# Query-key scores on one core: blocks of 8 heads, loads of 64 partitions of 8 KB, three output buffers

## The chip, the cores and the metric

One core of a Trainium2 chip. The metric is the device time of one execution in microseconds, the median of several runs. The granted TensorE clock was 1.0 in every profile.

Names used below, with what nearly all the work of each is on the page of the kernel before: PE multiplies matrices (1536 MATMUL at L159), DVE (vector) transposes (92 STREAM_TRANSPOSE), ACT (scalar) copies PE's results into the output buffers (379 COPY o_sb<-ps at L170), POOL casts (352 CAST at L115), and SP issues transfers (the 96 stores and a few first loads). A partition is one of the 128 rows of a tile (128x2048 in a copy of ACT); a packet is one transfer in the profile's records of the sixteen DMA engines (28248 in the kernel before).

## The reference

```python
batch, n_heads, seq, head_dim = 8, 12, 1024, 64
def reference(q, k):                      # float32
    return np.einsum('bhid,bhjd->bhij', q, k)
```

There are 96 heads. Each reads 2 x 256 KB and writes 4 MB.

## The kernel before

Heads are worked in blocks: two of 2 heads, then blocks of 4 (two "halves" of GMAX = 2 heads). For each block, q and k are loaded in rows of 4 KB per partition, cast to fp16 on POOL, transposed on DVE, multiplied on PE, evicted by ACT into an output buffer of 32 KB per partition, and stored with one 4 MB DMA per head.

```python
GMAX = 2
sizes = [1, 1] + [GMAX] * (BH // (2 * GMAX) - 1)
in_pool   = ...tile_pool(name="in_pool", bufs=5)
half_pool = ...tile_pool(name="half_pool", bufs=2)
out_pool  = ...tile_pool(name="out_pool", bufs=4)
...
def load(self, n, eng):                       # one of q, k for one half of a block
    half, x = divmod(n, 2)
    ...
    eng.dma_start(out=self.raw[half][:, x],   # 128 partitions x 4 KB
                  in_=src.rearrange("(p r) d -> p (r d)", p=P))
...
for i, b in enumerate(blocks):
    for n in range(2 * b.G):
        b.scores(n, side)                     # matmuls, evictions, store; side: DVE transposes
        if i == n == 0:
            next_load(nc.scalar)
        next_load(nc.scalar)                  # one load per head, on ACT's queue
    ...to_half(i + 3)                         # casts
```

The first three blocks' inputs share one output buffer ("early"). Stores go out on SP's queue, loads on ACT's (a few at the start on SP's).

## Time and profile before

| | before |
|---|---|
| time, first three runs | 1068.19 us |
| span of the profiled run | 1066.3 us |
| DMA, both data queues | 99.3% of 16 engines |
| busiest compute engine (PE) | 66% |
| store of 4 MB, issue to landing | 36.6 us |
| load of 512 KB, issue to landing | 34.3 us |

The page gives, for forty slices of the span, the busy tenths of each engine and the GB/s moved; then the DMA queues, the chain of work that ended last, and groups of instructions. The stretches used below (a view of chosen windows) end in three columns: granted clock, DMA share, GB/s. Two stretches of the kernel before are the yardstick: 12 to 22 us, where loads run almost alone, and 300 to 600 us, steady state.

```profile
12.00:22.00 10.00, 7.52 (x18) 2.54 (x17) 4.81 (x4) 5.50 (x6) 9.57 (x11) 1.00 1.03 410
...
300.00:600.00 300.00, 196.13 (x432) 65.99 (x432) 117.44 (x27) 197.43 (x109) 111.24 (x108) 1.00 1.01 431
```

The reader is to see 410 GB/s and 431 GB/s, both with the DMA engines all busy.

### The profile page before, as it was taken

What the parts mean: (1) busy time and instruction counts of PE and PEld (TensorE: products, weight loads), DVE (VectorE), ACT (ScalarE), POOL (GpSimd) and SP (SyncE); (2) the same over time, 40 slices, a digit from 0 to 9 for tenths busy, and PEclk for the clock granted to TensorE, in tenths of its full rate; (3) what the DMA queues carried; (4) which work ended last, traced back from release to release, by engine and by line L of the source; (5) the groups of instructions that cost most, each with busy time, mean ns of one, the idle gap of its engine ahead of it and who ended that gap; (6) DMA issues with size and microseconds to landing.
All of it is one profiled execution on the core that took longest, in us unless ns stands there. A gap on an engine that the chain in (4) does not pass through costs nothing.

```text
span 1066.3 us, 4563 instructions
## 1 busy us (share of the span) xinstructions
PE 701.0 (66%) x1568; PEld 237.4 (22%) x1568; DVE 417.4 (39%) x101; ACT 694.5 (65%) x384; POOL 385.7 (36%) x382
## 2 busy tenths in 40 slices
PE   5997757576675766757666675666757667678750
PEld 2332222222221222222222221222212222222210
DVE  3856516236063360633606336063360632624000
ACT  2897666675766757667576666756667576777750
POOL 7794333433334333343334433344333443300000
DMA  9999999999999999999999999999999999999995
GB/s 386 418 433 428 434 431 431 429 435 427 434 429 434 426 434 428 437 423 437 428 433 427 435 427 432 429 434 427 435 426 436 426 434 437 430 433 431 432 433 247
DMA packets 28248, 453.29 MB, mean 425 GB/s; under 512 B 3136, under 2 KB 3136, under 8 KB 15936
## 3 DMA queue, kind: packets, MB, share of 16 engines
q1 hardware_dynamic: 15120, 406.33, 88.5%
q10 hardware_dynamic: 13104, 46.67, 10.8%
q8 instruction: 12, 0.20, 0.1%
q14 instruction: 12, 0.10, 0.0%
HBM read 50.33 MB, written 402.65 MB: 425 GB/s over the span
## 4 chain that ended last, share of the span: by engine, by line
DMA 76%; ACT 13%; PE 6%; DVE 1%; issue 0%; ACTq 0%; SPq 0%
DMA out_dram<-o_sb 72%; ACT o_sb L170 13%; PE ps L159 6%; DMA x_sb<-in_q_dram 3%; DMA early<-in_k_dram 1%; DVE o_sb L166 0%; DVE o_sb L168 0%; ACT o_sb L165 0%; PE ps L140 0%; ACT L165 0%; DVE kT L143 0%; ACTq L170 0%; ACTq L74 0%; SPq L174 0%
## 5 line engine op out<-in xcount | busy, mean ns | idle before, releaser
L159 PE MATMUL ps<-kT,qT 64*128 64x512 f16 x1536 | 697.2, 617 | 321.9 <-ACT o_sb L170 316.6
L170 ACT COPY o_sb<-ps 128x2048 f32<-128x2048 f32 x379 | 689.3, 1869 | 324.7 <-DMA out_dram<-o_sb 297.0
L115 POOL CAST half_sb<-x_sb 32x1024 f16<-32x1024 f32 x352 | 363.8, 1033 | 531.4 <-DMA x_sb<-in_k_dram 512.5
L132 DVE STREAM_TRANSPOSE qT<-half_sb 128x1024 f16<-128x1024 f16 x46 | 214.3, 4659 | 533.5 <-issue 533.5
L159 PEld LDWEIGHTS <-qT 64*128 64x128 f16 x1536 | 234.1, 157 | 783.1 <-issue 780.2
L132 DVE STREAM_TRANSPOSE kT<-half_sb 128x1024 f16<-128x1024 f16 x46 | 216.1, 4697 | 0.0
L115 POOL CAST half_sb<-early 32x1024 f16<-32x1024 f32 x16 | 16.5, 1033 | 2.4 <-DMA early<-in_k_dram 1.7
L140 PE MATMUL ps<-ident,half_sb 128*128 128x128 f16 x32 | 3.9, 309 | 8.8 <-POOL half_sb L93 6.1
L165 ACT ACT_TABLE_LOAD x1 | 1.3, 1283 | 11.4 <-DMA early<-in_k_dram 11.4
L166 DVE COPY o_sb<-ps 128x1024 f32<-128x1024 f32 x4 | 4.8, 1223 | 6.5 <-ACT o_sb L165 6.5
L93 POOL CAST half_sb<-early 128x512 f16<-128x512 f32 x8 | 4.7, 613 | 3.3 <-DMA early<-in_q_dram 3.2
L165 ACT COPY o_sb<-ps 128x1024 f32<-128x1024 f32 x4 | 4.0, 1014 | 3.0 <-PE ps L159 3.0
L143 DVE COPY qT<-ps 128x1024 f16<-128x1024 f16 x2 | 2.5, 1225 | 8.3 <-PE ps L140 8.3
L140 PEld LDWEIGHTS <-half_sb 128*128 128x128 f16 x32 | 3.3, 142 | 10.3 <-POOL half_sb L93 6.1
L143 DVE COPY kT<-ps 128x1024 f16<-128x1024 f16 x2 | 2.4, 1220 | 3.6 <-PE ps L140 3.6
L168 DVE COPY o_sb<-ps 128x2048 f32<-128x2048 f32 x1 | 2.3, 2292 | 2.0 <-PE ps L159 2.0
masks.py:199 POOL TENSOR_SCALAR_AFFINE_SELECT ident<-ident 128x128 f16<-128x128 f16 x1 | 0.3, 292 | 0.1
masks.py:197 POOL MEMSET ident<- 128x128 f16 x1 | 0.2, 204 | 0.3 <-POOLq L266 0.3
L266 POOL MEMSET const-float32-0.0<- 128x1 f32 x1 | 0.1, 98 | 0.2 <-issue 0.2
L266 POOL MEMSET const-bfloat16-1.0<- 128x1 bf16 x1 | 0.1, 101 | 0.0
L266 POOL MEMSET const-uint8-127<- 128x1 uint8 x1 | 0.1, 101 | 0.0
L266 POOL MEMSET const-float32-1.0<- 128x1 f32 x1 | 0.1, 98 | 0.0
## 6 DMA issues: line engine op xcount, KB each, us to landing
out_dram<-o_sb SPq DMA_DIRECT2D x96, 4096.0 KB, 36.6
x_sb<-in_k_dram ACTq DMA_DIRECT2D x44, 512.0 KB, 34.4
x_sb<-in_q_dram ACTq DMA_DIRECT2D x41, 512.0 KB, 34.3
x_sb<-in_q_dram SPq DMA_DIRECT2D x3, 512.0 KB, 10.2
early<-in_k_dram ACTq DMA_DIRECT2D x4, 256.0 KB, 5.0
early<-in_q_dram SPq DMA_DIRECT2D x4, 256.0 KB, 4.6
early<-in_q_dram SPq DMA_DIRECT2D x2, 512.0 KB, 7.2
early<-in_k_dram ACTq DMA_DIRECT2D x2, 512.0 KB, 7.3
```

Source lines behind the costliest of these rows:

```text
L93: nc.gpsimd.tensor_copy(out=self.halves[x][:, :, half], in_=self.raw[half][:, x].rearrange("p (r d) -> p r d", d=D),)
L115: nc.gpsimd.tensor_copy(out=dst[:, :, b], in_=raw[32 * b : 32 * b + 32, :, :, h],)
L132: pin(nc.vector.transpose(out=dst[:, two], in_=src[:, two]))
L140: pin(nc.tensor.transpose(t_ps[:, t], self.halves[x][:, t], ident))
L143: pin(nc.vector.tensor_copy(out=dst, in_=src))
L159: nc.tensor.matmul(ps[:, tt, js], qT[cs, g, 2 * u + tt], kT[cs, g, js])
L165: pin(nc.scalar.copy(out=dst[:, 0], in_=ps[:, 0]))
L166: pin(nc.vector.tensor_copy(out=dst[:, 1], in_=ps[:, 1]))
L168: pin(nc.vector.tensor_copy(out=dst, in_=ps))
L170: pin(nc.scalar.copy(out=dst, in_=ps))
L266: nc = _bacc.Bacc("TRN2", target_bir_lowering=False, num_devices=1)
```

## The change

The intent is fewer and larger pieces: rows of 8 KB per partition, so half as many load packets, and half as many casts and transposes. The input and fp16 buffers grow, and one of the four output buffers goes. A load stays at 512 KB by being cut in two halves of 64 partitions. The core of the diff, with cuts marked:

```diff
-    GMAX = 2
+    GMAX = 4
-    sizes = [1, 1] + [GMAX] * (BH // (2 * GMAX) - 1)
+    sizes = [1, 1, 2] + [GMAX] * (BH // (2 * GMAX) - 1)
-    in_pool = ...bufs=5    half_pool = ...bufs=2    out_pool = ...bufs=4
+    in_pool = ...bufs=3    half_pool = ...bufs=3    out_pool = ...bufs=3
...
+        def pieces(self):
+            parts = 2 if self.G == GMAX else 1
+            return [(n, part, parts) for n in range(4) for part in range(parts)]
...
+            rows = slice(part * P // parts, (part + 1) * P // parts)
             pin(
                 eng.dma_start(
-                    out=self.raw[half][:, x],
-                    in_=src.rearrange("(p r) d -> p (r d)", p=P),
+                    out=self.raw[half][rows, x],
+                    in_=src.rearrange("(p r) d -> p (r d)", p=P)[rows],
                 )
             )
...                          (casts and transposes: same form, twice the columns)
-            if i == n == 0:
+            for _ in range(2 if b.first + n in (0, 2, 3, 4, 5) else 1):
                 next_load(nc.scalar)
-            next_load(nc.scalar)
...
+            to_half(i + 2 + (n == heads - 1))
```

More of the change, by code (lines that the diff above doesn't have):

```diff
@@ L45 @@
     ident = consts.tile([P, P], F16)
-    in_pool = ctx.enter_context(tc.tile_pool(name="in_pool", bufs=5))
-    half_pool = ctx.enter_context(tc.tile_pool(name="half_pool", bufs=2))
+    in_pool = ctx.enter_context(tc.tile_pool(name="in_pool", bufs=3))
+    half_pool = ctx.enter_context(tc.tile_pool(name="half_pool", bufs=3))
     tr_pool = ctx.enter_context(tc.tile_pool(name="tr_pool", bufs=2))
-    out_pool = ctx.enter_context(tc.tile_pool(name="out_pool", bufs=4))
+    out_pool = ctx.enter_context(tc.tile_pool(name="out_pool", bufs=3))
     po_pool = ctx.enter_context(
@@ L62, in __init__, with load @@
             self.raw = [None] * 2
-        def load(self, n, eng):
+        def pieces(self):
+            parts = 2 if self.G == GMAX else 1
+            return [(n, part, parts) for n in range(4) for part in range(parts)]
+        def load(self, piece, eng):
+            n, part, parts = piece
             half, x = divmod(n, 2)
@@ L97, in cast_rows, with cast_quads @@
                 )
-        def cast_quads(self, half_sb):
-            self.half_sb = half_sb
-            for half in range(2):
-                raw = self.raw[half].rearrange(
-                    "p x (r h d) -> p x r h d", h=2, d=32
-                )
-                for h in range(2):
-                    q0 = 32 * (2 * half + h)
-                    dst = half_sb[q0 : q0 + 32].rearrange(
-                        "p (x b r d) -> p x b r d", x=2, b=4, d=32
-                    )
-                    for b in range(4):
-                        pin(
-                            nc.gpsimd.tensor_copy(
-                                out=dst[:, :, b],
-                                in_=raw[32 * b : 32 * b + 32, :, :, h],
-                            )
+        def cast_quads(self, half):
+            raw = self.raw[half].rearrange("p x (r h d) -> p x r h d", h=2, d=32)
+            for h in range(2):
+                q0 = 32 * (2 * half + h)
+                for b in range(4):
+                    dst = self.half_sb[b // 2][q0 : q0 + 32].rearrange(
+                        "p (x b r d) -> p x b r d", x=2, b=2, d=32
+                    )
+                    pin(
+                        nc.gpsimd.tensor_copy(
+                            out=dst[:, :, b % 2],
+                            in_=raw[32 * b : 32 * b + 32, :, :, h],
                         )
+                    )
         def alloc(self):
@@ L125, in transpose_quads @@
         def transpose_quads(self, part, x):
-            src = self.half_sb.rearrange("p (x n) -> p x n", x=2)[:, x]
-            src = src.rearrange("p (b r i) -> p b r i", b=4, i=32)
-            dst = (self.qT, self.kT)[x].rearrange(
+            src = self.half_sb[part].rearrange(
+                "p (x b r i) -> p x b r i", x=2, b=2, i=32
+            )[:, x]
+            dst = (self.qT, self.kT)[x][:, : self.G * S].rearrange(
                 "c (b i r) -> c b r i", b=4, i=32, r=self.R
-            )
-            two = slice(2 * part, 2 * part + 2)
-            pin(nc.vector.transpose(out=dst[:, two], in_=src[:, two]))
+            )[:, 2 * part : 2 * part + 2]
+            pin(nc.vector.transpose(out=dst, in_=src))
         def transpose_rows(self, x):
@@ L197 @@
             at += 2 * b.elems
-        for n in range(4):
-            b.load(n, (nc.sync, nc.scalar)[n % 2])
-    stream = [(b, n) for b in blocks[3:] for n in range(4)]
+        for n, piece in enumerate(b.pieces()):
+            b.load(piece, (nc.sync, nc.scalar)[n % 2])
+    stream = [(b, piece) for b in blocks[3:] for piece in b.pieces()]
     def next_load(eng):
         if stream:
-            b, n = stream.pop(0)
-            b.load(n, eng)
+            b, piece = stream.pop(0)
+            b.load(piece, eng)
     for n in range(6):
@@ L209, with half_tile, to_half @@
     make_identity(nc, ident)
-    def to_half(i):
-        if i < len(blocks):
-            if i == 1:
-                half_sb = blocks[0].half_sb[:, 4 * blocks[0].elems :]
-            else:
-                half_sb = half_pool.tile([P, 8 * GMAX * NT * D // 2], F16, tag="half")
-            if i < PE_BLOCKS:
-                blocks[i].half_sb = half_sb
-                blocks[i].cast_rows(half_sb)
-            else:
-                blocks[i].cast_quads(half_sb)
-    for i in range(3):
-        to_half(i)
+    def half_tile():
+        half_sb = half_pool.tile([P, 2 * GMAX * NT * D], F16, tag="half")
+        return half_sb
+    casts = [(i, half) for i in range(PE_BLOCKS, len(blocks)) for half in range(2)]
+    def to_half(last):
+        while casts:
+            i, half = casts[0]
+            b = blocks[i]
+            if i > last:
+                return
+            if any(sb is b and piece[0] // 2 == half for sb, piece in stream):
+                return
+            if half == 0:
+                b.half_sb = [half_tile()[:, : 2 * b.elems] for _ in range(2)]
+            b.cast_quads(half)
+            casts.pop(0)
+    half_sb = half_tile()
+    at = 0
+    for b in blocks[:PE_BLOCKS]:
+        b.cast_rows(half_sb[:, at:])
+        at += 4 * b.elems
+    to_half(2)
     blocks[0].alloc()
@@ L240 @@
                 parts = [(p, x) for p in range(2) for x in range(2)]
-                each = 4 // heads
-                some = parts[n * each : (n + 1) * each]
+                some = [s for m, s in enumerate(parts) if m * heads // 4 == n]
                 side = {0: lambda: [nxt.transpose_quads(*s) for s in some]}
             b.scores(n, side)
-            if i == n == 0:
+            for _ in range(2 if b.first + n in (0, 2, 3, 4, 5) else 1):
                 next_load(nc.scalar)
-            next_load(nc.scalar)
-            if i == 0 and n == heads - 1:
-                to_half(3)
-        if i > 0:
-            to_half(i + 3)
+            to_half(i + 2 + (n == heads - 1))
 _INS = ['q', 'k']
```

## The prediction

> **What bounds the kernel now.** I read the page first, from its second part down. The kernel moves 453 MB (402.65 MB of it output, which no change can shrink), and the row of the DMA says that the sixteen DMA engines are at nine tenths or more in every slice but the last:
>
> ```profile
> DMA  9999999999999999999999999999999999999995
> GB/s 386 418 433 428 434 431 431 429 435 427 434 429 434 426 434 428 437 423 437 428 433 427 435 427 432 429 434 427 435 426 436 426 434 437 430 433 431 432 433 247
> ...
> q1 hardware_dynamic: 15120, 406.33, 88.5%
> q10 hardware_dynamic: 13104, 46.67, 10.8%
> ...
> DMA 76%; ACT 13%; PE 6%; DVE 1%; issue 0%; ACTq 0%; SPq 0%
> ```
>
> Queue 1 carries the stores (88.5% of the time of 16 engines), queue 10 the loads (10.8%): 99.3% together. No compute engine is above 66% on the same page. The chain of waits agrees, and shows how the buffers couple to it. Columns are start, length in us, what:
>
> ```profile
> 138.55 3.65 ACT o_sb L170 x2
> 142.21 36.10 DMA out_dram<-o_sb
> 178.33 0.04 ACTq L170
> 178.37 0.04 issue
> 178.41 1.88 ACT o_sb L170
> 180.29 0.04 issue
> 180.33 1.88 PE ps L159 x4
> 182.23 3.65 ACT o_sb L170 x2
> 185.89 36.13 DMA out_dram<-o_sb
> ```
>
> The reader is to see: a head is filled in 7.5 us (178.41 to 185.89), its 4 MB store then needs 36.1 us to land because three stores stand in line, and only then is its buffer filled again; the period of 43.68 us is four heads, 10.92 us each. Filling is short beside queueing, so the queue is never empty, and the chain names DMA. The waits say the same of the engines:
>
> ```profile
> POOL half_sb L115 <- DMA x_sb<-in_k_dram: 512.5, 38, 14.0
> PE ps L159 <- ACT o_sb L170: 316.6, 187, 4.2
> ACT o_sb L170 <- DMA out_dram<-o_sb: 297.0, 87, 4.2
> ```
>
> POOL waits half of the run for loads, ACT 297 us for store landings. None of these engines sets the end.
>
> I then went through the trace's single packet records. A store is 128 packets of 32 KB, 1213 ns each in the median; a 512 KB load is 128 packets of 4 KB, 159 ns each (5th to 95th percentile 159 to 164). The two sizes give a straight line: 28,672 B more cost 1054 ns, so 27.2 bytes/ns, and 159 - 4096/27.2 = 8.4 ns fixed per packet. Engines don't finish together: completions of the last store come at 1052 to 1056 us for most, but 1059.7, 1061.1 and 1064.4 us for three. The instruction fetches (twelve of 16 KB, 0.94 us each, 11 us in sum if they all fall on one engine) would explain the last[...].
>
> [...] from some 52 us on, the 4 KB packets are spread evenly in time, one beside each 32 KB one, and a load needs 34.3 us to land although its bytes are worth 1.3 us. [...] Every load of the kernel before has 128 partitions and none was slow, so its trace says nothing on this; it is the main doubt about the change.
>
> **The change, part by part.**
>
> 1. Loads. From the fourth block on there are 88 of 512 KB in both kernels; the bytes are the same. Packets go from 128 of 4 KB to 64 of 8 KB each. Per engine: 88 x 8 = 704 packets become 352, each pair saving 8.4 ns: 352 x 8.4 ns = 3.0 us. It is on the bounding engine, so the full 3.0 us count. That is all that the larger packet can give: 0.28%.
>
> 2. Casts. 352 casts of 1024 elements (1033 ns) become 176 of 2048. From 613 ns at 512 and 1033 at 1024 elements, 0.82 ns per element: about 1.87 us each, 330 us in place of 364. POOL is idle two thirds of the time: worth 0 on the path.
>
> 3. Transposes. 92 of 4.66 to 4.70 us become 4 of these and 44 of twice the size, about 9.3 us: 428 us against 430. DVE 39% busy: 0. A block's four take 37 us out of 87 us that eight heads last.
>
> 4. Output buffers. In the steady state a store landing at T lets ACT fill until T + 7.6 us, and the packets start some 2 us later. With three buffers two other stores, 22 us of work, are in line at T. The fastest engines are ahead of the slowest by up to 10 us at the end, so they have 12 us left against 9.6 needed: just enough, and idling of an engine that is ahead costs nothing anyway. I put 0 to 1 us. At the start one of three buffers holds the first loads, so the third head waits for the third block's casts, which end at 28.3 us; the first eviction of that head came at 34.3 us. 0 us. The landing of a store should fall from 36 us to about 26.
>
> 5. Waits of the loads on ACT's queue. A load into a reused input buffer waits for the casts of its earlier contents. Counting heads by the program's order, casts are through some four heads before the reuse in the steady state. At the start the fourth block's casts wait for DVE's transposes of the third (32.2 to 41.5 us in the trace before), so one load may hold ACT up to about 5 us near 50 us; two stores are in line then. 0 to 2 us.
>
> 6. Fewer instructions (44 on DVE, 176 on POOL) save a few instruction fetches of 309 ns: at most 1 us.
>
> Sum [...]: 1068.2 - 3.0 + 1 = about 1066 us.
>
> **The rivals.** [...] I give a visible effect (over 21 us) somewhat over a third.
>
> Second, store starvation by three buffers: if filling plus issue took longer than what is in line, DMA would dip in each head. The 7.5 us and 22 us above speak against; it would need a loss of 0.22 us in each of 96 heads to reach 2%. If it came, 1080 to 1090 us.
>
> Third, ACT held by the waits of loads, if loads land late: a loss in bursts at block ends, ACT's queue as releaser. Against it are the four heads of slack; for it, that slow loads under the first rival would eat it. Up to 10 us.
>
> A gain over 2% would need 21 us; the packets give 3, and even all engines ending together, at about 1055 us, would not.
>
> **Range and chances.** The likeliest outcome is 1063 to 1068 us[...]. I predict 1067 us, the main mode and a little for the tail; 1061 to 1125 us should hold it 8 times in 10[...]. Faster by over 2%: 0.02. Within 2%: 0.60. Slower: 0.38.
>
> **What will show it.** Load packets of 8 KB at 310 ns with the DMA row at nine tenths: step 1 right[...]. Load packets at 400 to 620 ns, GB/s falling to 370 to 410 while loads run and back to 432 in the last 150 us where none do[...]. DMA share below 0.95 with ACT's wait for store landings still large: the buffers. ACT's queue in the chain of waits at the loads' line: step 5. The store's landing near 26 us shows step 4. I am wrong above all [...] if three buffers leave engines idle in the steady state.

What is cut from the prediction, and marked, is an account of why loads of 64 partitions might be slow, with the estimates built on it, and a clause on whose instructions are fetched: no trace or run of this case shows them. Of the rivals, the first is that such loads are slow; "says nothing on this" means on loads of 64 partitions, since all loads of the kernel before have 128 (159 ns per 4 KB packet). The sum came to about 1066 us and has no term for this rival. The 64 us that I estimated for it (1130 us in all) are among the cut terms; the predicted 1067 us is the sum with a little for that tail, which also sets the upper end of 1125 us. The signs named for it (400 to 620 ns, 370 to 410 GB/s) stand as forecasts.

## The result and the profile after

The changed kernel took 1078.71 us (1077.51 to 1079.73, 6 runs) against 1068.21 us for before (1067.86 to 1068.87, 6 runs). The ratio is 1.0097, 95% interval 1.0084 to 1.0110: within 2%, but clearly slower. Ratios here are the mean time of one kernel's fast runs over that of the other's fast runs of the same rounds, so not quite the ratio of the medians.

The page of the changed kernel: GB/s by slice, the queues, the engines of the chain.

```profile
DMA  9999999999999999999999999999999999999996
GB/s 295 425 429 429 434 429 429 428 430 426 429 421 427 427 423 427 427 427 427 425 429 420 426 425 431 429 423 435 422 426 429 430 430 434 432 432 429 432 434 290
...
q1 hardware_dynamic: 14928, 406.33, 88.7%
q10 hardware_dynamic: 7664, 46.67, 10.7%
...
DMA 73%; ACT 17%; PE 7%; DVE 1%; issue 0%; ACTq 0%
```

The DMA engines are still always busy, yet the first slice falls from 386 to 295 GB/s, and those from the second to the last but one lie at 420 to 435 instead of 418 to 437. The queue of the loads has 7664 packets in place of 13104 for the same 46.67 MB. The DMA engines are busy and move less, so the loss is not one of waiting for a compute engine or a buffer. The two stretches say how much (windows of the changed kernel):

```profile
12.00:22.00 10.00, 6.28 (x16) 2.01 (x15) 4.80 (x4) 5.23 (x5) 9.61 (x10) 1.00 1.03 286
...
300.00:600.00 300.00, 195.40 (x431) 66.60 (x431) 117.59 (x13) 196.42 (x108) 100.87 (x55) 1.00 1.00 426
```

The load-only stretch runs at 286 instead of 410 GB/s at the same DMA share, 1.03. The steady state loses 1%. The large waits of the compute engines have moved little from those in the prediction (columns: time in all, times, longest, in us):

```profile
POOL half_sb L118 <- DMA x_sb<-in_k_dram: 488.6, 35, 22.5
PE ps L162 <- ACT o_sb L173: 334.1, 187, 4.8
ACT o_sb L173 <- DMA out_dram<-o_sb: 311.7, 91, 4.8
...
ACT o_sb L173 <- POOL half_sb L118: 4.0, 1, 4.0
```

ACT waits 15 us more for stores to land; the profiled run is 9.8 us longer. The last line is the one wait that the new order adds on ACT: it is held for 4 us by POOL's casts near 52 us, while the window from 50 to 60 us shows 432 GB/s, so no loss shows there. (POOL and DVE have some new waits for each other as well, 29 us in sum; neither engine is on the chain above for more than 1%.) The DMA issues (KB, then us from issue to landing) show three buffers and the quicker loads:

```profile
out_dram<-o_sb SPq DMA_DIRECT2D x96, 4096.0 KB, 25.6
x_sb<-in_k_dram ACTq DMA_DIRECT2D x43, 512.0 KB, 12.4
x_sb<-in_q_dram ACTq DMA_DIRECT2D x42, 512.0 KB, 12.5
```

The trace's single packet records complete it. Between 200 and 850 us a load packet of 8 KB took 310 ns in the mean, just as the straight line in the prediction has it. But the 32 KB store packets, untouched by the change, rose from 1215 to 1231 ns; 14% of them took over 1240 ns, before 1.5%. Sorted by how many load packets of all engines they overlapped, store packets with none took 1214 ns and those with 16 and more 1245 ns; in the kernel before the latter took 1216 ns. Before the first stores (12 to 21 us) the 8 KB load packets themselves took 479 ns.

To see where the loss falls I use one number from the same records: the time at which 128 x (n + 1) store packets had ended, less the same time of the kernel before.

| us behind before, one profile each | head 8 | head 75 | head 94 | steady part (75 less 8) |
|---|---|---|---|---|
| changed kernel | 11.1 | 17.9 | 12.5 | 6.8 |
| e1, 128 partitions x 4 KB | 5.4 | 5.2 | 1.4 | -0.2 |
| e2, 128 partitions x 8 KB | 5.9 | 6.3 | 0.6 | 0.4 |
| e3, before with three buffers | 0.5 | 0.4 | 0.9 | -0.1 |
| e5, fourth block 128, rest 64 | 7.2 | 14.4 | 9.2 | 7.2 |
| e6, fourth block 64, rest 128 | 11.4 | 11.0 | 5.8 | -0.4 |
| e7, 64 partitions x 4 KB | 22.2 | 32.7 | 26.9 | 10.5 |
| e8, lower half only | 11.5 | 19.6 | 14.4 | 8.1 |

In the changed schedule loads run ahead of before: some 5 us at head 8 are loads made early and come back when the loads end, after head 75, as e1 shows. The steady part is free of that. The repeats e9 and e10 below give 1.3 and -0.5 us in the last column for the kernels of e2 and e1, so differences of about 1 us there mean nothing.

### The profile page after: what moved, and what is told of

It is laid out like the page before. It is cut to its first block, busy times and chain, and to the rows that moved or that the text cites. A ratio compares the mean times of both kernels' runs of the same rounds, so it can differ in the third digit from the quotient of the medians.

```text
span 1076.1 us, 4312 instructions
## 1 busy us (share of the span) xinstructions
PE 700.7 (65%) x1568; PEld 240.4 (22%) x1568; DVE 429.0 (40%) x57; ACT 694.5 (65%) x384; POOL 354.1 (33%) x206
## 3 DMA queue, kind: packets, MB, share of 16 engines
q10 hardware_dynamic: 7664, 46.67, 10.7%
## 4 chain that ended last, share of the span: by engine, by line
DMA 73%; ACT 17%; PE 7%; DVE 1%; issue 0%; ACTq 0%
DMA out_dram<-o_sb 72%; ACT o_sb L173 16%; PE ps L162 6%; DMA early<-in_k_dram 1%; DVE o_sb L169 0%; DVE o_sb L171 0%; PE ps L143 0%; ACT o_sb L168 0%; ACTq L81 0%; ACT L168 0%; DVE kT L146 0%; DVE qT L146 0%; ACTq L173 0%
## 5 line engine op out<-in xcount | busy, mean ns | idle before, releaser
L118 POOL CAST half_sb<-x_sb 32x2048 f16<-32x2048 f32 x176 | 332.1, 1887 | 525.4 <-DMA x_sb<-in_k_dram 488.6
L162 PEld LDWEIGHTS <-qT 64*128 64x128 f16 x1536 | 237.1, 157 | 799.8 <-issue 797.5
L135 DVE STREAM_TRANSPOSE qT<-half_sb 128x2048 f16<-128x2048 f16 (+1 forms) x24 | 214.0, 8916 | 479.1 <-issue 459.3
L135 DVE STREAM_TRANSPOSE kT<-half_sb 128x2048 f16<-128x2048 f16 (+1 forms) x24 | 216.8, 9035 | 0.0
L146 DVE COPY kT<-ps 128x1024 f16<-128x1024 f16 x2 | 2.4, 1220 | 4.9 <-PE ps L143 4.9
## 6 DMA issues: line engine op xcount, KB each, us to landing
out_dram<-o_sb SPq DMA_DIRECT2D x96, 4096.0 KB, 25.6
x_sb<-in_q_dram ACTq DMA_DIRECT2D x42, 512.0 KB, 12.5
```

The lines of the kernel that those rows point to most:

```text
L118: nc.gpsimd.tensor_copy(out=dst[:, :, b % 2], in_=raw[32 * b : 32 * b + 32, :, :, h],)
L135: pin(nc.vector.transpose(out=dst, in_=src))
L146: pin(nc.vector.tensor_copy(out=dst, in_=src))
L162: nc.tensor.matmul(ps[:, tt, js], qT[cs, g, 2 * u + tt], kT[cs, g, js])
```

## The experiments

Theory: the loads' 64 partitions are the cause, by whatever mechanism. It has a cost at the start, where loads run alone, and one in the steady state. No run shows a mechanism. Where [...] stands before an outcome in e1, e2, e3 and e5, that outcome is the one of this theory. In the first sentences of e2, e7 and e10 it stands for a clause of the same account. Rivals: three output buffers; the larger blocks with their waits; the 8 KB packet itself. In e1 to e8 the kernels share the runs of before (1068.58 us, 11 runs, for e1, e2, e3, e5; 1068.36 us, 9 runs, for e6 to e8).

### e1: the same kernel, loads of 128 partitions again

```diff
-            rows = slice(part * P // parts, (part + 1) * P // parts)
+            cols = slice(part * self.elems // parts, (part + 1) * self.elems // parts)
...
-                    out=self.raw[half][rows, x],
-                    in_=src.rearrange("(p r) d -> p (r d)", p=P)[rows],
+                    out=self.raw[half][:, x, cols],
+                    in_=src.rearrange("(p r) d -> p (r d)", p=P)[:, cols],
```

> The changed kernel with each load cut along its columns in place of its partitions: 128 partitions of 4 KB, as before the change; blocks, casts, transposes, three buffers and the number of loads stay. [...] the whole loss goes, 1068 us (1066.5 to 1069.5), packets of 32 KB back to a mean near 1215 ns and the first loads back to 410 GB/s. Buffers theory (three instead of four, or the waits of larger blocks): it stays at 1077 to 1079 us.

Measured: 1069.20 us (5 runs), ratio 1.0006 (0.9994 to 1.0018). Windows of this run:

```profile
12.00:22.00 10.00, 7.35 (x18) 2.38 (x16) 4.81 (x4) 5.50 (x6) 9.61 (x10) 1.00 1.02 390
...
300.00:600.00 300.00, 197.08 (x435) 67.09 (x434) 131.34 (x15) 197.34 (x109) 105.64 (x56) 1.00 1.01 431
```

Both stretches are back (390 and 431 GB/s), store packets at 1214.6 ns. 9.5 of the 10.5 us go with the shape of the loads alone. Larger blocks, double casts and transposes and three buffers together cost about a microsecond; the intervals here and in e10 allow up to 3 us. The order in which the source is read is no rival either: the changed kernel reads each 512 KB in one piece, as before, and e1, which reads them in 4 KB pieces with gaps, is fast.

### e2: 128 partitions of 8 KB, 1 MB per load

```diff
+            if part:
+                return
...
-            rows = slice(part * P // parts, (part + 1) * P // parts)
+            rows = slice(0, P)
```

> The changed kernel with loads of 128 partitions of 8 KB, 1 MB each, one every second head[...]. [...] the packet arithmetic: 1068.2 - 3.0 = 1065 us (1064 to 1066.5), the fastest of all. If packets of 8 KB themselves disturb the stores (they hold an engine twice as long between two store packets), it stays near 1075 to 1079 us. Buffers theory: 1077 to 1079 us.

Measured: 1066.50 us (1065.38 to 1071.80, 6 runs), ratio 0.9987 (0.9973 to 1.0002). Windows of this run:

```profile
12.00:22.00 10.00, 8.51 (x20) 2.67 (x19) 5.05 (x5) 5.61 (x5) 9.61 (x10) 1.00 1.02 422
...
300.00:600.00 300.00, 197.09 (x435) 67.18 (x434) 112.77 (x13) 197.37 (x109) 97.52 (x52) 1.00 1.00 430
```

Between 12 and 21 us its 8 KB load packets took 315 ns, against 479 ns in the changed kernel. So the 8 KB packet is not what slows the changed kernel, though it holds an engine twice as long (309 ns against 159 in the medians of the changed kernel and of the one before). The expected 3 us are there at most in part: store packets took 1220 ns in the mean against 1215, and 768 of them per engine times 5 ns would be 3.8 us. Why they lengthen here, with all 128 partitions in use, no run tells.

### e3: the kernel before with three output buffers

```diff
-    out_pool = ctx.enter_context(tc.tile_pool(name="out_pool", bufs=4))
+    out_pool = ctx.enter_context(tc.tile_pool(name="out_pool", bufs=3))
```

> The kernel before with three output buffers instead of four and nothing else. [...] within 0.15% of before, 1067 to 1069.5 us, the landing of a store down from 36.6 to about 26 us. Buffers theory: most of the loss appears here, 1074 to 1079 us.

Measured: 1068.07 us (5 runs), ratio 1.0000 (0.9988 to 1.0012). The issues of this run:

```profile
out_dram<-o_sb SPq DMA_DIRECT2D x96, 4096.0 KB, 25.6
x_sb<-in_k_dram ACTq DMA_DIRECT2D x44, 512.0 KB, 23.3
```

A store lands after 25.6 us instead of 36.6, because two stand in line instead of three, and the time is the same. The buffers theory falls.

### e5: only the fourth block's loads at 128 partitions

```diff
+            if self.first == 8:
+                rows = slice(0, P)
+                cols = slice(part * self.elems // parts, (part + 1) * self.elems // parts)
+            else:
+                rows = slice(part * P // parts, (part + 1) * P // parts)
+                cols = slice(0, self.elems)
```

> The changed kernel with 128 partitions of 4 KB in the eight loads of the fourth block only (six of them run alone before the first store); the other 80 stay at 64 partitions. [...] what the start costs goes, 5 to 6 us, the rest stays: 1073 us (1071.5 to 1074.5). If the loss is in the steady state alone: 1077 to 1079 us; if it is the start alone: 1066 to 1068 us.

Measured: 1075.40 us (1073.57 to 1076.58, 5 runs), ratio 1.0058 (1.0045 to 1.0071). 3.3 us come back, somewhat less than expected. The start runs at 384 GB/s again, the steady state stays slow:

```profile
12.00:22.00 10.00, 7.44 (x18) 2.48 (x17) 4.80 (x4) 5.50 (x6) 9.57 (x11) 1.00 1.01 384
...
300.00:600.00 300.00, 194.76 (x430) 66.35 (x429) 114.50 (x13) 193.84 (x108) 98.71 (x53) 1.00 1.00 425
```

### e6: the complement

The edit is that of e5 with `self.first != 8`.

> The complement of the run before: loads of 64 partitions of 8 KB in the fourth block alone, 128 partitions of 4 KB in the other 80. If the costs of start and steady state add, it has what the start costs over the all-128 version (1069.2 us): the run before gave back 3.3 us of 1078.7, so 1072.5 us (1071 to 1074), with the later stretch at 431 GB/s. If the start is made up for later, 1069 to 1070 us.

Measured: 1073.71 us (5 runs), ratio 1.0052 (1.0039 to 1.0064). It lies 4.5 us over e1, and e5 6.2 us over e1: 10.7 in sum against the 9.5 of both together, so the two costs about add. The windows are the mirror of those of e5:

```profile
12.00:22.00 10.00, 6.88 (x17) 2.24 (x16) 4.80 (x4) 5.50 (x6) 9.61 (x10) 1.00 1.03 261
...
300.00:600.00 300.00, 196.14 (x432) 66.81 (x432) 120.86 (x14) 197.65 (x109) 105.64 (x56) 1.00 1.01 431
```

### e7: 64 partitions with 4 KB packets

```diff
+            w = self.elems // parts
+            for c in range(parts):
+                cols = slice(c * w, (c + 1) * w)
                 ... dma_start(out=self.raw[half][rows, x, cols], in_=...[rows, cols])
```

> The changed kernel with each load of 64 partitions of 8 KB issued as two of 64 partitions of 4 KB[...]. The start should lose the same as in the changed kernel (some 3.3 to 5.6 us). In the steady state, [...] 7 us become about 4, in all 1069.2 + 3.3 + 4 = 1076 us. [...] 7 us stay, 1069.2 + 3.3 + 7 = 1079.5 us. If the 8 KB packets were the cause and not the partitions, 1069 to 1070 us.

The first two sums are for 64 partitions as the cause, with a steady loss of 4 or 7 us: 4 if load packets delay one another, 7 if they delay stores.

Measured: 1088.79 us (1086.60 to 1090.20, 4 runs), ratio 1.0190 (1.0176 to 1.0204). None of the three was right. Part of it is made by my edit: twice as many loads near the start hold ACT's queue, and the DMA runs half empty for a while (window of this run):

```profile
90.00:100.00 10.00, 7.38 (x17) 2.48 (x17) 10.00 (x3) 8.97 (x6) 8.74 (x5) 1.00 0.56 126
```

So the total does not test the theory. The steady part is 10.5 us, more than the 6.8 of the changed kernel, but some of that is still the start: between heads 8 and 20, 3.3 us are lost (0.7 in the changed kernel), and the windows of 160 to 180 and 200 to 220 us show 411 and 409 GB/s. From head 20 to head 75 it is 7.2 us against 6.1 in the changed kernel and 6.0 in e5, while the versions with 128 partitions lie between -0.9 and 0.6. So e7 loses no less than 8 KB packets do, and no clear surplus is shown. Load packets are stretched here: 159 ns in the median but 294 ns at the 95th percentile of the whole run (239 ns between 200 and 850 us); with 128 partitions (e1) these are 165 and 159 ns. With e1 and e2 all four pairings of 64 or 128 partitions with 4 or 8 KB have been run: both of 64 are slow (between 12 and 22 us e7 moves 282 GB/s, like the changed kernel's 286) and both of 128 are not, so the number of partitions is the cause and the size of the packet is not. The expectation's 4 us failed, and its 7 us fits the later heads; but as the reasons for either size were not shown, e7 does not tell whether load packets delay one another or stores.

### e8: all later loads into partitions 0 to 63 (wrong result)

```diff
+            to = slice(0, 64) if self.first > 8 else rows
-                    out=self.raw[half][rows, x, cols],
+                    out=self.raw[half][to, x, cols],
...
+                    c = b % 2 if self.first > 8 else b
-                            in_=raw[32 * b : 32 * b + 32, :, :, h],
+                            in_=raw[32 * c : 32 * c + 32, :, :, h],
```

> Wrong result on purpose. Base is the version with the fourth block at 128 partitions (1075.4 us); all later loads of 64 partitions go to partitions 0 to 63, also those meant for 64 to 127, and the casts read there. Same bytes, packets and order. [...] 1075.4 us (1073.5 to 1077). [...] twice the 7 us, 1082 us (1080 to 1086).

The first outcome is for a loss that does not depend on which half the loads go to, the second for one that is then twice the 7 us.

Measured: 1079.00 us (1077.99 to 1079.75, 4 runs), between the two. The second load into the same rows must wait for the first, which holds ACT's queue in the first 100 us (ACT idles for 10.5, 7.2 and 5.5 us); head 8 comes 4.3 us later than in e5 (11.5 against 7.2), and that is all of the difference (3.6 us in the medians). The steady part is 8.1 us against 7.2 in e5, not the 14 of the second outcome. That count takes all engines together, though, and could hide a lag of some of them. The sixteen completions of each store settle part of it: between heads 8 and 75 the last of them falls 7.6 us further behind (e5: 6.6) and the first 5.2 (e5: 7.1), neither near 14. But they also split in two: at head 75 nine lie within 1.8 us and the other seven 8.2 to 11.5 us after the first, a gap of 6.3 us where the largest in e5 is 2.0. Some of the engines do lag somewhat. So with all loads in one half the steady part is about that of e5, and not twice that, with one profile each and an artefact at the start; whether load packets delay one another or stores this run does not show.

### e9 and e10: the two 128-partition versions once more

The kernels are those of e2 and e1 without an edit.

> The version with loads of 128 partitions of 8 KB once more, because its first five rounds gave 0.9987 of before with an interval that just reaches 1. If the packets' arithmetic holds (3.0 us off, part of it given back by slower store packets: 1220 against 1215 ns in the mean), 0.997 to 0.9995 of before with an interval below 1; if the first result was noise, 1.000.

> The version with loads of 128 partitions of 4 KB once more, beside the other on the same chip: blocks of eight heads, double casts and transposes, three buffers[...]. If these parts cost nothing, within 0.1% of before (first result 1.0006); the other version 2 to 3 us below it.

Measured, with before at 1068.37 us (10 runs): e9 1067.38 us (1065.78 to 1071.00, 6 runs), ratio 1.0001 (0.9984 to 1.0017); e10 1069.44 us (6 runs), ratio 1.0015 (1.0003 to 1.0028). The gain of e2 was not reproduced: its median lies 1 to 2 us below before both times, but its single runs scatter from 1065.4 to 1071.8 us, and no gain is shown. The rest of the change (blocks, three buffers, order of loads) costs some 0.1%, by the interval of e10 at most 0.3%.

## Why the prediction was right or wrong

The range (1061 to 1125 us) and the most likely class (within 2%) held. The predicted time, 1067 us, was 11.7 us too low, and the direction was wrong: it took the main case to be one without a loss by the 64 partitions. That the class held is in part luck: its reason, no such loss, did not come true; one of 9.5 us by the shape of the loads, which lies between the two cases that the prediction weighed (none, and 21 us or more), did.

**Step 1, load packets: the size right, the gain not realised.** The 8 KB packets took 309 to 310 ns as the line said. But no version with 8 KB packets was measurably faster than before; e2 and e9 have 0.9987 and 1.0001. The term "3.0 us" assumed that the store packets would keep their 1213 ns.

**Steps 2 and 3, casts and transposes: right.** Groups of the changed kernel by form (columns as in the fifth part of the page):

```profile
L118 POOL CAST half_sb<-x_sb 32x2048 f16<-32x2048 f32 x176 | 332.1, 1887 | 525.4 <-DMA x_sb<-in_k_dram 488.6 <-issue 17.0 <-DVE kT L135 9.3
L135 DVE STREAM_TRANSPOSE kT<-half_sb 128x2048 f16<-128x2048 f16 x22 | 207.4, 9427 | 0.0
L135 DVE STREAM_TRANSPOSE qT<-half_sb 128x2048 f16<-128x2048 f16 x22 | 204.7, 9306 | 479.1 <-issue 459.3 <-POOL half_sb L118 19.9
```

A cast took 1.89 us (1.87 predicted), a transpose 9.3 to 9.4 us (9.3 predicted), and neither is on the path.

**Step 4, buffers: right.** The landing fell to 25.6 us (26 predicted), and e3 shows a ratio of 1.0000.

**Step 5, waits of loads: right.** Casts held ACT once, for 4.0 us (up to 5 predicted), near 52 us, without a gap in the DMA. **Step 6** can't be told apart from noise; the small instruction fetches fell from 12 to 10 (q14 on the pages).

**The first rival, slow loads of 64 partitions, is the one that fits what the runs show, and its size was the mis-sized term.** The signs that I named were half right. "Load packets at 400 to 620 ns" is what the start showed (479 ns); in the steady state the load packets kept 310 ns and the store packets beside them grew by 16 ns. "GB/s falling to 370 to 410" was too much: 426. My estimate of 64 us rested on a mechanism that no run shows and on engines that stay at one phase for the whole run; the measured steady part was 6.8 us. Nothing supports a fixed phase: the completions of one store are spread over 0.7 us at the first head but over 2.7 us at head 8 and 10.4 us at head 75 of the kernel before (2.8 and 9.3 us in the changed kernel), so engines drift apart by several times the 1.52 us that a store and a load packet take (1.21 + 0.31). What the packet records alone give, as an estimate: 16 ns more for each of the 8 store packets per engine and head are 8.6 us in the 67 heads from 8 to 75; four load packets in place of eight save 2.3 us there, by the prediction's 8.4 ns; 6.3 us remain, measured 6.8. That says where the steady part lies, in longer store packets, not why. Why the 4 us in my expectation for e7 failed is not shown.

**What was left out: the start.** The prediction put the cost of such loads into the steady state only. Six loads of the fourth block run before the first store: 261 and 286 GB/s against 384 to 427 where that block has 128 partitions, and load packets of 523 (e6) and 479 ns. That part is 3.3 to 4.5 us of the loss, the steady part the other 6 us or so.

**Open:** why loads of 64 partitions are slow. The runs show that the number of partitions is the cause; no run shows the mechanism. Whether a load of 64 partitions taken in part from each half of the 128 is slow too was not run. Open too: how much comes from load packets that delay stores, and how much from those that delay one another (e7, e8); whether the store packet that grows is the one behind a slow load packet on the same engine (the records do not carry the engine); why store packets grow somewhat (1220 to 1223 ns) beside 8 KB loads of 128 partitions; and whether the twelve instruction fetches of 16 KB (0.88 to 1.06 us each) explain that in the kernel before the last store's completions lie 12 us apart (1052 to 1064 us).

## What to carry to other kernels

Where the DMA engines bound a kernel, as here, look at a load's number of partitions before its packet size: cut along the columns (e1) or left whole (e2) the loads cost a microsecond or nothing, cut along the partitions 9.5 us, though the packets of e1 are half as long. Look at GB/s at a DMA share of 1.0, not at the share, which was 1.03 both at 410 and at 286 GB/s, and read it in a stretch where loads run alone. And before estimating from a worst case that lasts the whole run, look in the trace whether it can last: the completions of one store were spread over 0.7 us at the first head and 10.4 us at head 75, and the worst case gave 64 us where 6.8 were measured.
